# Two transformer layers on one core: GLA's backward pass handed out over attention heads

## The chip, the cores and the metric

One Trainium2 chip, one of its cores. The metric is device time of one execution in microseconds, as a median over runs. The engines are TensorE (PE, with its weight load as PEld), VectorE (DVE), ScalarE (ACT), GpSimd (POOL) and SyncE (SP), which issues most of the transfers.

## The reference

Two layers over 2048 latent tokens and 256 context tokens of width 1024. Each layer normalizes, projects to 3104 columns, lets four head groups work side by side, gates each, and projects back:

```
pl = split_proj(h_l @ w_in);  pc = split_proj(h_c @ w_in)
a = gla_mixer(...)      # gated linear attention, both directions
b = fourier_mix(...)    # 2-D Fourier transform, then w_f
c = swa_mixer(...)      # banded attention: 128-token blocks, neighbours, context, a sink logit
d = na_mixer(...)       # neighbourhood attention on the 32 x 64 grid, plus context
x = x + gate * (concat([a*silu(a_g), b*silu(b_g), c*silu(c_g), d*silu(d_g)]) @ w_out)
```

GLA runs a recurrence `S_t = diag(a_t) S_{t-1} + k_t^T v_t`, `o_t = q_t S_t` forward and backward over context and latent tokens, adds the two outputs, and takes an RMS norm per head of 64.

## The kernel before

All is fp32. Projections split each operand into a high and a low part and sum three matmuls (`mm3`, lines 218 to 222): their PSUM tiles are `ps` (input projections) and `pso` (output projection). The 2304 tokens are 9 pieces `s` of 256, or 18 tiles `T` of 128; the pieces go in three groups T1 = 0, 1, 2; T2 = 3, 4, 5; T3 = 6, 7, 8.

A layer (`trunk`, from line 1198) projects group by group and runs GLA's forward direction and the local part of both (`gla_fast`). For each tile it leaves in HBM a record `so[T]` of 642 columns: the output so far (0 to 256), the backward update (256 to 512), the decayed queries (512 to 640) and two decays. `gla_guard` then reads a flag and branches (line 639) past a slow path. After it:

- `gla_bwd` (line 646) walks the 18 tiles from the last to the first, context ahead. A tile's record `brec` is loaded; the state `sbk` of the tiles gone by is scaled (`sbe`, DVE), multiplied by the queries (`pob`, PE, in the one PSUM tile of tag `y`), added to the output (DVE). Then come a square (`bsq`, ACT), a sum (`gss`) and a scale (`ms`, both DVE), a power (`rs`, POOL, line 191), the norm's weight (`won`, POOL), a product (`bsq`, DVE), two transposes (`pyt`, PE, a tile of the two-buffered PSUM pool of tag `m`), a copy (`by`, ACT) and a store. One more DVE operation carries the state on. In layer 1 the two context tiles only carry the state on.
- `fnet` (line 689) transforms the Fourier group: 16-point transforms on DVE (`fft16`, lines 765 to 806, tiles `v`, `sd`, `fo`), then matmuls `px` into `XT`, then `pab` into `yT`.
- the last two projections of T3, `cq` and `dq` (`pst` are their transposes).
- `attention` (line 1181) takes a list of phases, makes one item of each head, and hands the items to `pipeline` (line 876), which places an item's parts a fixed number of items apart: `load`, scores `pse` (PE) in a single PSUM tile of tag `s`, bias and minimum (`S`, `am`, DVE), exponential (`S`, ACT), transposes `ppt` (PE, tag `m`), their copies `pt`, and for two heads together `py` (PE, tag `y`), which DVE scales into `yt`. Between heads stand items that project gates (`chunks`), reload (`redo`) or project out (`out_proj`). Layer 0 has 144 heads, layer 1 has 128.

Order on an engine is set by a scheduler: it takes what the program wrote first and lets later work that is ready fill the gaps. So projections, which come later in the program, stand between the pieces of GLA, FNet and the heads. At run time each engine keeps that order. `gla_bwd` and `fnet` share one pool, opened at line 1232 and closed before attention's.

Of the kernel before, what the change touches and what calls it, by code (L numbers as in the profile page):

```python
# [8 lines left out]
F32 = mybir.dt.float32  # L9
# [28 lines left out]
class Kern:  # L38
# [605 lines left out]
                    self.gla_slow(L, s, pool, lmask)  # L644

    def gla_bwd(self, L, pool):
        nc = self.nc
        sb = None
        won = pool.tile([128, 256], F32, tag="won", name="won", bufs=1)
        nc.sync.dma_start(won, self.a["won"][L].rearrange("(o d) -> o d", o=1).to_broadcast([128, 256]))  # L650
        for T in [1, 0] + list(range(17, 1, -1)):
            full = not (T < 2 and L == 1)
            rec = pool.tile([128, 644], F32, tag="brec", name="brec", bufs=4)
            if full:
                nc.sync.dma_start(rec[:, 0:642], self.so[T][:, 0:642])
            else:
                nc.sync.dma_start(rec[:, 256:512], self.so[T][:, 256:512])
                nc.sync.dma_start(rec[:, 640:642], self.so[T][:, 640:642])
            if full:
                o = rec[:, 0:256]  # L660
                if sb is not None:
                    po = self.py.tile([128, 512], F32, tag="y", name="pob")
                    sbe = pool.tile([128, 256], F32, tag="sbe", name="sbe", bufs=2)
                    nc.vector.tensor_scalar(out=sbe, in0=sb, scalar1=rec[:, 640:641], scalar2=None, op0=ALU.mult)
                    nc.tensor.matmul(po[:, 0:256], rec[:, 512:640], sbe, start=True, stop=True)
                    nc.vector.tensor_tensor(out=o, in0=po[:, 0:256], in1=o, op=ALU.add)
                sq = pool.tile([128, 256], F32, tag="bsq", name="bsq", bufs=3)
                nc.scalar.activation(out=sq, in_=o, func=AF.Square)
                ss = self.sm.tile([128, 4], F32, tag="gss", name="gss")
                nc.vector.tensor_reduce(out=ss, in_=sq.rearrange("p (h d) -> p h d", d=64), op=ALU.add, axis=AX.X)  # L670
                rs = self.rstd(ss, 4, 1.0 / 64, "g")
                nc.gpsimd.tensor_tensor(out=o, in0=o, in1=won, op=ALU.mult)
                nc.vector.tensor_tensor(out=sq.rearrange("p (h d) -> p h d", d=64), in0=o.rearrange("p (h d) -> p h d", d=64),
                                        in1=rs.rearrange("p (h o) -> p h o", o=1).to_broadcast([128, 4, 64]), op=ALU.mult)
                pt = self.pm.tile([128, 512], F32, tag="m", name="pyt")
                for b in range(2):
                    nc.tensor.transpose(pt[:, b * 128:b * 128 + 128], sq[:, b * 128:b * 128 + 128], self.idn)
                y = pool.tile([128, 2, 128], F32, tag="by", name="by", bufs=2)
                nc.scalar.copy(y, pt[:, 0:256].rearrange("p (b c) -> p b c", b=2))
                nc.sync.dma_start(self.y[L][T // 2][:, 0:2, (T % 2) * 128:(T % 2) * 128 + 128], y)  # L680
            s2 = pool.tile([128, 256], F32, tag="sbk", name="sbk", bufs=2)
            if sb is None:
                nc.vector.tensor_copy(out=s2, in_=rec[:, 256:512])
            else:
                nc.vector.scalar_tensor_tensor(out=s2, in0=sb, scalar=rec[:, 641:642], in1=rec[:, 256:512], op0=ALU.mult, op1=ALU.add)
            sb = s2


    def fnet(self, L, pool, ctx):
# [160 lines left out]
    def transpose_p(self, pool, S, n, rc=None):  # L850

        nc = self.nc
        out, rt = [], None
        for c0 in range(0, n, 3):
            w = min(3, n - c0)
            p = self.pm.tile([128, 4, 128], F32, tag="m", name="ppt")
            pt = pool.tile([128, 3, 128], F32, tag="pt", name="pt", bufs=10)  # L860
            for i in range(w):
                nc.tensor.transpose(p[:, i], S[:, (c0 + i) * 128:(c0 + i + 1) * 128], self.idn)  # L862
            if rc is not None and c0 + w == n:
                rd = pool.tile([128, 2, 64], F32, tag="rd", name="rd", bufs=2)
                nc.gpsimd.tensor_copy(out=rd, in_=rc.rearrange("p (h o) -> p h o", o=1).to_broadcast([128, 2, 64]))
                nc.tensor.transpose(p[:, 3], rd.rearrange("p h d -> p (h d)"), self.idn)
                rt = pool.tile([128, 128], F32, tag="rt", name="rt", bufs=2)
                nc.scalar.copy(rt, p[:, 3])
            if c0:
                nc.scalar.copy(pt[:, 0:w], p[:, 0:w])  # L870
            else:
                nc.vector.tensor_copy(out=pt[:, 0:w], in_=p[:, 0:w])  # L872
            out += [pt[:, i] for i in range(w)]
        return out, rt
# [306 lines left out]
    def attention(self, L, *phases):  # L1181


        with self.tc.tile_pool(name=f"at{L}", bufs=2) as p:
            items, self.bias = [], {}
            for ph in phases:
                if ph is None:
                    items += self.na_ctx_rows(L, p)
                elif isinstance(ph, int):
                    items += self.na(L, p, ph)  # L1190
                elif isinstance(ph, tuple):
                    run, nop = lambda f=ph[1]: f(), lambda *r: None
                    items.append((None, run, nop) if ph[0] == "before" else (None, nop, lambda r, x, f=ph[1]: x == 2 and f()))
                elif ph:
                    items += self.swa(L, p, ph)
            self.pipeline(items)

    def trunk(self):
        tc = self.tc
        first, kv, gates = ["av", "lr", "aqk"], ["bv", "ckv", "dk", "dv"], ["ag", "bg", "cg", "dg"]  # L1200
        for L in range(2):
# [28 lines left out]
            self.gla_guard(L)  # L1230
            kc.close()
            with tc.tile_pool(name=f"gb{L}", bufs=2) as p:
                self.gla_bwd(L, p)
                self.fnet(L, p, False)
            self.chunks(L, T3, ["cq", "dq"], h, ws)
            hs = {}
# [6 lines left out]
            b, f = (lambda f, *a: ("before", lambda: f(*a))), (lambda f, *a: ("after", lambda: f(*a)))  # L1243
# [139 lines left out]
```

## Time and profile before

| | us |
|---|---|
| median of 3 runs | 2963.52 |
| lowest and highest | 2957.93, 2965.28 |
| profiled execution, own time | 2951.03 |
| its span, first to last instruction | 2949.1 |
| PE busy | 2718.3 |
| DVE busy | 1609.3 |
| mean granted PE clock (share of 2.4 GHz) | 0.959 |

The profile is of one execution. Busy shares are means over stages that have different limits, so it is read by stretches: in layer 0 PE stops at the guard's branch at 615 us, the first `pab` of FNet starts at 723, the first `pse` at 773, the last `pse` ends near 1434; in layer 1 the same points are near 2099, 2213, 2264 and 2834.

### The profile page before, as it was taken

The numbers are of one execution on the slowest core, as the hardware profiler recorded it, in microseconds if no ns is written. First come the engines' busy times: TensorE is split into PE (matmuls) and PEld (weight loads), VectorE is DVE, ScalarE is ACT, GpSimd is POOL, SyncE is SP. The second block draws the span as 40 slices with busy tenths as digits, with TensorE's granted clock in tenths as the row PEclk, the third lists the DMA queues.
The fourth block names the chain that finished last, engine by engine and source line by source line (L and its number), as shares of the span: only waits on it lengthen the run. The fifth ranks groups of instructions, "written<-read, shape, count | busy, mean of one in ns | idle before, by whom it ended". The sixth has DMA issues, their size and how long they took to land. (4 is left out here: it accounts for less than half of the span.)

```text
span 2949.1 us, 55777 instructions
## 1 busy us (share of the span) xinstructions
PE 2718.3 (92%) x21206; PEld 2410.2 (82%) x21206; DVE 1609.3 (55%) x3741; ACT 1070.9 (36%) x2344; POOL 837.3 (28%) x922
## 2 busy tenths in 40 slices
PE   5989988988999999999959889999879999999998
PEld 5889878976888778887859889889768888878788
DVE  7554775557355454645484553464483646455543
ACT  3333323322344343344224323334232444444432
POOL 3233222234132121312133332332351313121222
PEclk9999988999999999999979999989999999999999
DMA  8635544245565274554464664333465654456545
GB/s 273 194 108 163 169 136 126 84 145 166 162 192 167 81 215 129 158 157 124 147 193 134 196 185 144 93 111 104 119 190 162 199 164 135 146 163 190 161 149 180
DMA packets 476681, 458.00 MB, mean 155 GB/s; under 512 B 54763, under 2 KB 355565, under 8 KB 476013
## 3 DMA queue, kind: packets, MB, share of 16 engines
q1 hardware_dynamic: 472782, 440.66, 48.9%
q0 software_dynamic: 3616, 13.64, 1.9%
q8 instruction: 170, 2.79, 0.4%
q14 instruction: 113, 0.93, 0.1%
HBM read 339.56 MB, written 114.60 MB: 154 GB/s over the span
## 5 line engine op out<-in xcount | busy, mean ns | idle before, releaser
L220 PE MATMUL ps<-whi,hh 128*128 128x256 f32 x1968 | 586.4, 298 | 34.7 <-ACT hh L258 17.2
L222 PE MATMUL ps<-whi,hl 128*128 128x256 f32 x1968 | 582.0, 296 | 10.2 <-DVE hl L259 10.2
L221 PE MATMUL ps<-wlo,hh 128*128 128x256 f32 x1968 | 580.8, 295 | 6.4 <-PEq L639 6.4
L213 POOL TENSOR_TENSOR wlo<-wraw,whi 128x512 fp32r<-128x512 f32 x208 | 280.8, 1350 | 775.7 <-ACT whi L212 735.1
L220 PEld LDWEIGHTS ps<-whi,hh 128*128 128x128 f32 x1968 | 391.9, 199 | 46.4 <-ACT hh L258 19.0
L220 PE MATMUL ps<-hh,whi 128*128 128x256 f32 x1376 | 402.5, 292 | 5.3 <-ACT ev L311 2.3
L222 PEld LDWEIGHTS ps<-whi,hl 128*128 128x128 f32 x1968 | 391.3, 199 | 18.5 <-DVE hl L259 13.9
L221 PE MATMUL ps<-hl,whi 128*128 128x256 f32 x1376 | 403.3, 293 | 0.0
L222 PE MATMUL ps<-hh,wlo 128*128 128x256 f32 x1376 | 402.4, 292 | 0.0
L221 PEld LDWEIGHTS ps<-wlo,hh 128*128 128x128 f32 x1968 | 392.4, 199 | 11.0 <-issue 8.8
L212 ACT CAST whi<-wraw 128x512 fp32r<-128x512 f32 x416 | 242.3, 620 | 378.5 <-DMA wraw<-w_in 206.9
L844 ACT ACTIVATE S<-S,am 128x641 f32<-128x641 f32 (+5 forms) x272 | 226.1, 831 | 339.1 <-DVE am L836 324.5
L220 PE MATMUL pso<-mh,whi 128*128 128x256 f32 x1088 | 316.7, 291 | 5.3 <-DVE xo L1107 2.9
L222 PE MATMUL pso<-mh,wlo 128*128 128x256 f32 x1088 | 316.2, 291 | 2.3 <-POOL wlo L213 1.8
L221 PE MATMUL pso<-ml,whi 128*128 128x256 f32 x1088 | 315.1, 290 | 0.0
L213 DVE TENSOR_TENSOR wlo<-wraw,whi 128x512 fp32r<-128x512 f32 x208 | 187.9, 907 | 170.9 <-ACT whi L212 163.4
L220 PEld LDWEIGHTS ps<-hh,whi 128*128 128x128 f32 x1376 | 265.9, 193 | 15.2 <-issue 7.9
L222 PEld LDWEIGHTS ps<-hh,wlo 128*128 128x128 f32 x1376 | 265.8, 193 | 15.1 <-issue 14.8
L221 PEld LDWEIGHTS ps<-hl,whi 128*128 128x128 f32 x1376 | 266.0, 193 | 11.4 <-issue 11.0
L830 PE MATMUL pse<-kst,q 64*128 64x256 f32 (+2 forms) x1184 | 246.6, 457 | 13.6 <-DVE am L836 12.5
L191 POOL TENSOR_TENSOR rs<-ms,mhalf 128x8 f32<-128x8 f32 (+2 forms) x140 | 171.3, 1226 | 297.5 <-DVE ms L189 288.6
L862 PE MATMUL ppt<-idn,S 128*128 128x128 f32 x1360 | 243.6, 284 | 10.4 <-DVE pt L872 5.2
(203 smaller groups left out, 4866.4 us busy)
## 6 DMA issues: line engine op xcount, KB each, us to landing
wraw<-w_in SPq DMA_DIRECT2D x288, 256.0 KB
wraw<-w_out SPq DMA_DIRECT2D x128, 256.0 KB
adaw<-ada_w SPq DMA_DIRECT2D x82, 256.0 KB
scr_g<-ev SPq DMA_DIRECT2D x68, 256.0 KB
g<-scr_g SPq DMA_DIRECT2D x34, 512.0 KB
y<-scr_y SPq DMA_DIRECT2D x34, 512.0 KB
bias<-nbias SPq DMA_DIRECT2D x48, 256.0 KB
scr_h<-x SPq DMA_DIRECT2D x22, 512.0 KB
```

Of the source, the lines that this page charges most:

```text
L191: nc.gpsimd.tensor_tensor(out=rs, in0=ms, in1=self.mhalf.to_broadcast([128, n]), op=ALU.pow)
L212: nc.scalar.copy(hi[:, k], raw)
L213: (nc.gpsimd if i % 4 else nc.vector).tensor_tensor(out=lo[:, k], in0=raw, in1=hi[:, k], op=ALU.subtract)
L220: nc.tensor.matmul(out, ah(k), bh(k), start=(k == 0), stop=False)
L221: nc.tensor.matmul(out, ah(k), bl(k), start=False, stop=False)
L222: nc.tensor.matmul(out, al(k), bh(k), start=False, stop=(k == KB - 1))
L830: nc.tensor.matmul(p[:, lo:hi], q[r], k, start=True, stop=True, tile_position=(64 * o, 0))
L844: nc.scalar.activation(out=S[:, 0:w], in_=S[:, 0:w], func=AF.Exp, scale=-1.0, bias=m[:, 0:1], accum_out=m[:, 1:2])
L862: nc.tensor.transpose(p[:, i], S[:, (c0 + i) * 128:(c0 + i + 1) * 128], self.idn)
```

## The change

`gla_bwd` no longer emits its 18 tiles at once. It returns 18 steps. A step loads the record of the next tile and computes its own; step 0 loads its own record too. `attention` hangs step k behind the last part of item 4k + 4, so that a step comes after every fourth item, from item 4 to item 72, in both layers. The tiles now come from attention's pool: `brec` has 2 buffers (was 4), `bsq` 2 (was 3), and `pt` of attention 9 (was 10). FNet stands alone in its pool. What is computed, and each instruction with its shape, is the same.

```diff
--- before.py
+++ after.py
@@ -644,19 +644,30 @@
                     self.gla_slow(L, s, pool, lmask)
 
     def gla_bwd(self, L, pool):
-        nc = self.nc
-        sb = None
+
+        nc = self.nc
+        st = {"sb": None, "rec": []}
         won = pool.tile([128, 256], F32, tag="won", name="won", bufs=1)
         nc.sync.dma_start(won, self.a["won"][L].rearrange("(o d) -> o d", o=1).to_broadcast([128, 256]))
-        for T in [1, 0] + list(range(17, 1, -1)):
+        tiles = [1, 0] + list(range(17, 1, -1))
+
+        def load(T):
             full = not (T < 2 and L == 1)
-            rec = pool.tile([128, 644], F32, tag="brec", name="brec", bufs=4)
+            rec = pool.tile([128, 644], F32, tag="brec", name="brec", bufs=2)
             if full:
                 nc.sync.dma_start(rec[:, 0:642], self.so[T][:, 0:642])
             else:
                 nc.sync.dma_start(rec[:, 256:512], self.so[T][:, 256:512])
                 nc.sync.dma_start(rec[:, 640:642], self.so[T][:, 640:642])
-            if full:
+            st["rec"].append(rec)
+
+        def step(n):
+            if n == 0:
+                load(tiles[0])
+            if n + 1 < len(tiles):
+                load(tiles[n + 1])
+            T, rec, sb = tiles[n], st["rec"].pop(0), st["sb"]
+            if not (T < 2 and L == 1):
                 o = rec[:, 0:256]
                 if sb is not None:
                     po = self.py.tile([128, 512], F32, tag="y", name="pob")
@@ -664,7 +675,7 @@
                     nc.vector.tensor_scalar(out=sbe, in0=sb, scalar1=rec[:, 640:641], scalar2=None, op0=ALU.mult)
                     nc.tensor.matmul(po[:, 0:256], rec[:, 512:640], sbe, start=True, stop=True)
                     nc.vector.tensor_tensor(out=o, in0=po[:, 0:256], in1=o, op=ALU.add)
-                sq = pool.tile([128, 256], F32, tag="bsq", name="bsq", bufs=3)
+                sq = pool.tile([128, 256], F32, tag="bsq", name="bsq", bufs=2)
                 nc.scalar.activation(out=sq, in_=o, func=AF.Square)
                 ss = self.sm.tile([128, 4], F32, tag="gss", name="gss")
                 nc.vector.tensor_reduce(out=ss, in_=sq.rearrange("p (h d) -> p h d", d=64), op=ALU.add, axis=AX.X)
@@ -683,7 +694,8 @@
                 nc.vector.tensor_copy(out=s2, in_=rec[:, 256:512])
             else:
                 nc.vector.scalar_tensor_tensor(out=s2, in0=sb, scalar=rec[:, 641:642], in1=rec[:, 256:512], op0=ALU.mult, op1=ALU.add)
-            sb = s2
+            st["sb"] = s2
+        return [lambda n=n: step(n) for n in range(len(tiles))]
 
 
     def fnet(self, L, pool, ctx):
@@ -857,7 +869,7 @@
         for c0 in range(0, n, 3):
             w = min(3, n - c0)
             p = self.pm.tile([128, 4, 128], F32, tag="m", name="ppt")
-            pt = pool.tile([128, 3, 128], F32, tag="pt", name="pt", bufs=10)
+            pt = pool.tile([128, 3, 128], F32, tag="pt", name="pt", bufs=9)
             for i in range(w):
                 nc.tensor.transpose(p[:, i], S[:, (c0 + i) * 128:(c0 + i + 1) * 128], self.idn)
             if rc is not None and c0 + w == n:
@@ -1193,7 +1205,15 @@
                     items.append((None, run, nop) if ph[0] == "before" else (None, nop, lambda r, x, f=ph[1]: x == 2 and f()))
                 elif ph:
                     items += self.swa(L, p, ph)
-            self.pipeline(items)
+            steps = {4 * k + 4: f for k, f in enumerate(self.gla_bwd(L, p))}
+
+            def wrap(i, item):
+                def last(r, x):
+                    item[2](r, x)
+                    if x == 2 and i in steps:
+                        steps[i]()
+                return item[0], item[1], last
+            self.pipeline([wrap(i, it) for i, it in enumerate(items)])
 
     def trunk(self):
         tc = self.tc
@@ -1230,7 +1250,6 @@
             self.gla_guard(L)
             kc.close()
             with tc.tile_pool(name=f"gb{L}", bufs=2) as p:
-                self.gla_bwd(L, p)
                 self.fnet(L, p, False)
             self.chunks(L, T3, ["cq", "dq"], h, ws)
             hs = {}
```

Three places in the order of instructions, before and after.

DVE, layer 0, inside FNet's second 16-point transform before the change (`sd`, `v` and `fo` are its tiles; `nsq` and `wlo` belong to projections):

```order
L765 TENSOR_TENSOR v<-v 128x128 x2
L765 TENSOR_TENSOR sd<-sd 128x384 x2
L664 TENSOR_SCALAR sbe<-sbk,brec 128x256
L685 SCALAR_TENSOR_TENSOR sbk<-sbk,brec 128x256
L189 TENSOR_SCALAR ms<-ss 128x8
L376 TENSOR_TENSOR nsq<-ps,wdq_897 128x512
L189 TENSOR_SCALAR ms<-gss 128x4
L666 TENSOR_TENSOR brec<-pob,brec 128x256
L213 TENSOR_TENSOR wlo<-wraw,whi 128x512
L795 TENSOR_SCALAR v<-sd 128x128
L768 SCALAR_TENSOR_TENSOR v<-sd 128x128
```

DVE, the first 16-point transform of layer 0 after the change:

```order
L777 TENSOR_TENSOR sd<-v 128x1024 x2
L777 TENSOR_TENSOR v<-sd 128x512 x2
L777 TENSOR_TENSOR v<-v 128x256
L777 TENSOR_TENSOR fo<-v 128x128 x2
L777 TENSOR_TENSOR v<-v 128x128 x2
L777 TENSOR_TENSOR sd<-sd 128x384 x2
L777 TENSOR_TENSOR fo<-v 128x128 x2
L780 SCALAR_TENSOR_TENSOR fo<-v 128x128 x4
L374 TENSOR_REDUCE ss<-nsq 128x8
L780 SCALAR_TENSOR_TENSOR v<-sd 128x128 x2
L807 TENSOR_SCALAR v<-sd 128x128
```

Of the eleven rows before, four are a GLA tile's; after the change the transform's rows follow one another with one row of a projection among them.

PE, some heads of layer 0, before (repeated `ps` rows left out):

```order
L830 MATMUL pse<-kst,q 128x384
L830 MATMUL pse<-kst,q 128x256
L862 MATMUL ppt<-idn,S 128x128 x3
L220 MATMUL ps<-hh_12562,whi 128x256
...
L220 MATMUL ps<-hh_12562,whi 128x256
L862 MATMUL ppt<-idn,S 128x128 x2
L866 MATMUL ppt<-idn,rd 128x128
L221 MATMUL ps<-hl_12563,whi 128x256
...
L221 MATMUL ps<-hl_12563,whi 128x256
L830 MATMUL pse<-kst,q 128x384
```

PE, layer 0 after the change, at the last block of window attention (heads 52 to 55):

```order
L878 MATMUL ppt<-idn,rd 128x128
L842 MATMUL pse<-kst,q 128x384
L842 MATMUL pse<-kst,q 128x256
L934 MATMUL py<-pt,vc 64x128 x4
L934 MATMUL py<-pt,vd 64x128 x4
L842 MATMUL pse<-kst,q 128x384
L842 MATMUL pse<-kst,q 128x256
L676 MATMUL pob<-sbe,brec 128x256
L688 MATMUL pyt<-idn,bsq 128x128 x2
L874 MATMUL ppt<-idn,S 128x128 x8
```

Before, twenty-odd and then nine `ps` stand between one `pse` and the next. Here there is none, and `pob` has `pyt` as its next neighbour, ahead of eight transposes of the heads.

PE, from the last `py` of layer 0 into layer 1, before (`p` is layer 1's norm; 204 `pso` from the first to the last):

```order
L922 MATMUL py<-pt,vd 64x128 x6
L220 MATMUL pso<-mh,whi 128x256
...
L222 MATMUL pso<-mh,wlo 128x256
L236 MATMUL p_18989<-ocol,sq 128x1
L240 MATMUL p_18989<-idn,rb 128x128
L236 MATMUL p_19016<-ocol,sq 128x1
L220 MATMUL ps<-whi,hh 128x256
```

PE, the same norm after:

```order
L220 MATMUL pso<-mh,whi 128x256
L236 MATMUL p_18989<-ocol,sq 128x1
L221 MATMUL pso<-ml,whi 128x256
...
L934 MATMUL py<-pt,vc 64x128 x4
L934 MATMUL py<-pt,vd 64x128 x6
L842 MATMUL pse<-kst,q 128x384
L842 MATMUL pse<-kst,q 128x256
L874 MATMUL ppt<-idn,S 128x128 x2
...
L240 MATMUL p_18989<-idn,rb 128x128
L222 MATMUL pso<-mh,wlo 128x256
```

Layer 1's first norms now stand among the last heads of layer 0, with `pso` between the two matmuls of one norm.

## Rows read from the trace of the kernel before

**Rows 1.** The page, part 1: busy us, share of the span, instructions.

```profile
PE 2718.3 (92%) x21206; PEld 2410.2 (82%) x21206; DVE 1609.3 (55%) x3741; ACT 1070.9 (36%) x2344; POOL 837.3 (28%) x922
```

**Rows 2.** Busy us of each engine by stretch (from:to, length), granted clock, DMA share.

```profile
615.00:723.00 108.00, 82.43 (x484) 72.81 (x484) 85.39 (x231) 27.48 (x65) 56.61 (x48) 0.89 0.61 182
...
2099.00:2213.00 114.00, 85.58 (x540) 76.66 (x539) 85.41 (x227) 27.77 (x66) 54.12 (x46) 0.90 0.60 174
...
760.00:1436.00 676.00, 659.51 (x5552) 551.74 (x5551) 353.78 (x841) 276.67 (x637) 155.87 (x238) 0.99 0.52 152
...
1472.00:1548.00 76.00, 43.67 (x292) 41.50 (x292) 61.96 (x134) 20.35 (x30) 29.25 (x28) 0.75 0.63 197
```

**Rows 3.** PE in order of time, layer 0: start, us, line, operation.

```profile
656.78 0.60 PE L725 MATMUL px<-T,fo 128*128 128x256 f32 x2
657.21 0.59 PE L723 MATMUL px<-T,fo 128*128 128x256 f32 x2
...
658.90 0.29 PE L222 MATMUL ps<-whi,hl 128*128 128x256 f32 x1
659.02 0.38 PE L677 MATMUL pyt<-idn,bsq 128*128 128x128 f32 x2
659.25 0.60 PE L665 MATMUL pob<-sbe,brec 128*128 128x256 f32 x2
659.68 0.38 PE L677 MATMUL pyt<-idn,bsq 128*128 128x128 f32 x2
```

**Rows 4.** PE's waits, 615 to 760: waiter, releaser; us, times, longest.

```profile
PE pyt L677 <- DVE bsq L673: 6.0, 4, 2.5
PE ps L221 <- PEq L639: 3.7, 1, 3.7
PE px L723 <- ACT XT L727: 3.6, 2, 2.1
PE pob L665 <- DMA brec<-scr_so: 3.5, 1, 3.5
```

**Rows 5.** PE's waits, 2098 to 2255.

```profile
PE pob L665 <- DVE brec L666: 12.2, 4, 5.3
PE pob L665 <- DMA brec<-scr_so: 4.7, 1, 4.7
PE pyt L677 <- DVE bsq L673: 3.2, 3, 1.9
```

**Rows 6.** DVE by group, 628 to 726: count, busy us, mean ns, idle before.

```profile
L673 DVE TENSOR_TENSOR bsq<-brec,rs 128x256 f32<-128x256 f32 x18 | 9.2, 509 | 2.9 <-POOL rs L191 2.9
...
L666 DVE TENSOR_TENSOR brec<-pob,brec 128x256 f32<-128x256 f32 x17 | 7.0, 411 | 2.3 <-PE pob L665 2.3
...
L189 DVE TENSOR_SCALAR ms<-gss 128x4 f32<-128x4 f32 x18 | 3.9, 218 | 0.1
```

**Rows 7.** Tile brec (min/median/max ns), then the page's part 5.

```profile
L668 ACT ACTIVATE bsq<-brec x34: 416/417/456, 628.2 to 2199.1; 128x256 f32<-128x256 f32 x34
...
L191 POOL TENSOR_TENSOR rs<-ms,mhalf 128x8 f32<-128x8 f32 (+2 forms) x140 | 171.3, 1226 | 297.5 <-DVE ms L189 288.6
```

**Rows 8.** All engines in order of time, attention of layer 0.

```profile
987.05 0.91 PE L830 MATMUL pse<-kst,q 64*128 64x384 f32 x4
...
988.11 0.88 DVE L836 CUSTOM_DVE_ANT_0 S<-pse,cmask,sink 128x640 f32<-128x640 f32 x1
...
995.48 0.91 PE L830 MATMUL pse<-kst,q 64*128 64x384 f32 x4
```

**Rows 9.** PE's waits, 1430 to 1560.

```profile
PE p L240 <- DVE rb L239: 10.2, 2, 6.0
PE ps L220 <- ACT hh L258: 5.7, 1, 5.7
PE p L236 <- DVE x L241: 5.3, 2, 3.1
```

**Rows 10.** PE's waits, 760 to 1120.

```profile
PE pse L830 <- DVE am L836: 4.8, 5, 1.6
```

## The prediction

> **What bounds the kernel now.** I read the page first. PE is busy for 92% of the span, no other engine for more than 55% [rows 1], so time is PE's work plus the moments in which PE has none. Next the table of stretches [rows 2], to see where PE loses time. In attention it loses little (layer 0: 659.5 us busy of 676). It loses much in the stretch that the change empties, from the guard to the first `pab` of FNet: 82.4 of 108 us busy in layer 0, 85.6 of 114 in layer 1, at granted clocks of 0.89 and 0.90. There DVE is the full engine: 85.4 of 108 and 85.4 of 114, against 353.8 of 676 in attention.
>
> How much PE loses there is worked out from starts of neighbouring matmuls, as a matmul's own duration includes its pipeline [rows 3]: a `ps` takes 0.12 us of PE (658.90 to 659.02), one pair of `px` 0.43, one `pob` 0.43, the two `pyt` 0.23. Layer 0 has 325 `ps` in the stretch (39.0), 32 `px` pairs (13.8), 17 `pob` (7.3), 16 pairs of `pyt` (3.7) and some 4 us of `pst` and `pg`: 68 us of work in 108, so **40 us lost**. Layer 1 likewise: 380 `ps` (45.6), 13.8, 16 `pob` (6.9), 3.7 and 4 make 74 in 114, again **40 lost**. PE's waits name about 26 and 28 us of it [rows 4, 5]; the rest is mostly the lower granted clock.
>
> Last, the waits: on the stretch's longest lists stand `pyt` behind DVE's `bsq` (6.0 us), `pob` behind the load of `brec` (3.5) in layer 0, `pob` behind DVE's `brec` (12.2) and its load (4.7), `pyt` (3.2) in layer 1 [rows 4, 5]. These are the GLA chain itself, and PE's queue is in order: what stands behind a late `pob` (the projections) waits too.
>
> **What is removed there.** Each tile puts six small operations on DVE. From 628 to 726 their six groups sum to 9.2 + 8.9 + 8.5 + 7.3 + 7.0 + 3.9 = 44.8 us busy of 86.2, first and last of them in [rows 6]; DVE overlaps neighbours a little, so some 31 to 45 us of DVE time leave each FNet stage, and with them 11 us of PE, 18 `brec` loads and 18 stores. FNet's transform then runs unbroken (first order fence). What stays are waits the change doesn't touch: the guard's branch (PE's queue, 3.7) and `px` behind XT (3.6) [rows 4].
> Bounds for the gain: at least the waits that name GLA's own tiles, 9.5 + 20.1 = 30 us; at most nearly all that is lost, 80 less the branch waits and a slow stretch behind each, about 65. I take 20 in layer 0 and 25 in layer 1: **45 us**, because DVE's other work in the stretch (about 41 us of the 86.2) then fits well beside PE's 60 to 70.
>
> **What is added in attention.** PE's 11 us per layer are the same work as before and cancel. Not cancelled is what the step does to the heads. In the new order a step is `pob`, then half a dozen items, then `pyt` standing ahead of the next heads' `ppt`. From `pob` to `pyt` runs DVE add 0.41, ACT square 0.42, DVE reduce 0.41 (7.3 over 18), `ms` 0.22, POOL pow 1.23, DVE multiply 0.51, together 3.2 us without hand-overs [rows 6, 7]. Usually 27 to 40 `ps` or `pso` (3.2 to 4.8 us), two `pse` and a `py` lie between, which covers it. With it go 18 loads and 18 stores per layer on SP's queue and two POOL operations per tile; POOL is busy for 156 of 676 us [rows 2], and no PE wait in attention names a `brec`-sized load, so I cost those at nothing; if SP's in-order queue holds up a `q` load, they turn up as `pse` behind a DMA. The smaller buffers (`brec` 2, `bsq` 2, `pt` 9) I also put at nothing: the load of tile n+1 waits for tile n-1, four heads back, and `pt` serves two tiles a head for three heads.
> For the 35 steps together, waits of `pob` and `pyt` lie between nothing and what these two cost beside FNet (30 us, above); I take **8**, since DVE is half idle here and a tile waits for DVE rather than for data.
>
> **Cover that is used up.** The filler between heads is finite. By the orders, layer 0 puts 598 `ps` between guard and last `pab` where it put 528, and 1053 instead of 833 under its first 48 heads; then about ten heads have almost none (second fence). Layer 1 runs short for about twelve heads late in attention. What such a head costs: two heads from 987.05 take 8.43 us until the `pse` at 995.48 [rows 8], with some 31 `ps` (3.7 us) between, so a head's own PE work is 2.35 us. The PSUM tile of the scores is single: `pse` at 987.05, DVE's reading of it (`S`, `am`) from 988.11 to 988.99, so the next `pse` could come after about 2.1 us instead of 4.2. Per bare head PE thus idles between 0 and 2.0 us (heads at 4.2 us as with filler, less 2.35, rounded up); I take 0.7, nearer the row, for 22 heads: **16 us**. Three GLA steps have little or nothing between `pob` and `pyt` either: 0 to 3.2 each, I take 2.5, near the chain's own length, as nothing else is left to run: **8 us**.
>
> **The layers' seam.** Because the filler is spent earlier, layer 0's projection of the first tokens now ends before its heads do. Before, 204 `pso` stand behind the last `py`, then layer 1's norms come with nothing beside them (third fence): PE 43.7 busy of 76 us at clock 0.75 [rows 2], with waits for `rb` (10.2), `hh` (5.7) and `x` (5.3) [rows 9], some 32 us of waits in all. Now the first three norms stand among the last heads. Between 0 and 32; I take **20 us**, as three of the six still run alone.
>
> **Sum.** -45 - 20 + 8 + 16 + 8 = **-33 us**. The profiled execution took 2951.0 us (span 2949.1), 12.5 us under the median of 2963.5; a difference carries over, so 2963.5 - 33 = **2930**.
>
> **Rivals.**
> *The heads absorb it.* By the table PEld is 551.7 of 676 us in attention, 82%, where PE is 98% [rows 2]: a busy PE there may still have room, and neither bare heads nor steps cost anything. Then -65, 2899. Against it: `pse` already waits for `am` (4.8 us in 360) [rows 10]. The Trainium skill ("Perfetto Trace Analysis", Identifying the Most-Contended Engine) says that weight-load busy time, not matmul busy time, tells PE's headroom; by it these 18% are real room and this rival's sum holds.
> *The heads stall (slower).* The place is the two-buffered pool of `pyt` and `ppt`: a `pyt` waiting for its DVE chain keeps the next heads' transposes behind it. It decides where filler is short, since then nothing fills the wait. Price: bare heads 22 x 2.0 = 44, three bare steps 8, the steps' waits as beside FNet 30, against -45 - 20: +17, **2980**. For it: under the first 48 heads the new order sets 22 `ps` to a head (1053 over 48) where it set 17. Against it: 8.43 us with only 4.7 of own work. The Trainium skill (same page, Optimization Strategy) reads a gap that repeats as too few buffers for the next tile; the old trace shows none such in attention (the longest is 4.8 us over five waits), so by that rule too it would have to be new.
> *Nothing is won.* FNet's stage keeps its pace through `px`, XT and loads of T, with more `ps` in it; only GLA's own waits go (-30), the seam stays, and the 32 us of costs come: +2, **2965**.
>
> **Chances.** Forecast 0.50, heads absorb 0.17, heads stall 0.17, nothing won 0.16. This kernel's measurement can't tell less than about 0.3% (9 us) from no change. The forecast's own range is 2908 to 2954; faster takes nearly all of it, all of the first rival and a little of the last: 0.66; no change 0.15; slower 0.19. The range leaves out a tenth on each side: 2897 to 2975.
>
> **What would show it.** Right: DVE below two thirds busy from guard to first `pab`, that stretch under 90 us in both layers, `sd` starting by itself; `pob` and `pyt` in attention with under 10 us of PE waits; the seam's waits at half. Wrong: PE waiting on `pyt`, or on `am` and `pt`, for 30 us or more where filler is missing; FNet's stretch still over 100 us; new waits of `pse` on DMA.

## The result and the profile after

The changed kernel takes 2996.02 us (median of four runs, 2991.27 to 3002.18), the kernel before 2961.47 beside it: ratio 1.0132, 95% interval 1.0105 to 1.0159. It is slower by 35 us where 33 us less were forecast, and lies above the range. The profiled execution's span is 2998.1 us (before 2949.1), the mean granted clock 0.951 (before 0.959).

The page's first part, after [rows 1]: PE is busy for 36 us more, though the kernel has the same 21206 matmuls.

```profile
PE 2754.6 (92%) x21206; PEld 2434.6 (81%) x21206; DVE 1601.2 (53%) x3741; ACT 1072.4 (36%) x2344; POOL 832.9 (28%) x922
```

Next the table of stretches (from:to, length, then busy us of PE, PEld, DVE, ACT, POOL, granted clock, DMA), cut at the same events in both kernels. After [rows 2]: guard to first `pab`, first to last `pse`, last `pse` to layer 1, then the first two for layer 1, and the end.

```profile
618.00:709.00 91.00, 73.80 (x491) 69.46 (x490) 48.93 (x129) 17.02 (x34) 20.91 (x15) 0.91 0.45 133
...
762.00:1508.00 746.00, 702.08 (x5694) 583.03 (x5694) 403.00 (x965) 293.08 (x674) 194.31 (x279) 0.96 0.52 151
1508.00:1630.00 122.00, 108.34 (x846) 104.70 (x844) 80.39 (x189) 41.63 (x78) 33.28 (x31) 0.93 0.62 194
2119.00:2203.00 84.00, 68.40 (x426) 61.84 (x425) 46.34 (x128) 15.87 (x31) 25.92 (x14) 0.88 0.46 134
...
2256.00:2921.00 665.00, 632.20 (x5206) 525.15 (x5208) 365.68 (x859) 273.09 (x622) 183.16 (x251) 0.97 0.57 167
2921.00:2998.00 77.00, 68.23 (x559) 65.59 (x559) 25.78 (x45) 18.37 (x33) 18.49 (x14) 0.98 0.50 156
```

Before, the stretches that [rows 2] don't have: heads of layer 0, the stretch behind them, heads of layer 1, the end.

```profile
773.00:1434.00 661.00, 644.72 (x5431) 537.36 (x5430) 348.91 (x835) 273.39 (x630) 150.58 (x231) 0.99 0.51 151
1434.00:1608.00 174.00, 141.64 (x1112) 138.31 (x1111) 98.27 (x215) 48.73 (x88) 48.54 (x45) 0.88 0.54 171
2264.00:2834.00 570.00, 561.03 (x4786) 461.71 (x4786) 315.65 (x740) 251.68 (x575) 139.57 (x212) 0.99 0.57 167
2834.00:2949.00 115.00, 105.58 (x870) 103.17 (x867) 43.08 (x65) 27.87 (x47) 30.20 (x21) 0.98 0.54 169
```

FNet's stretches are shorter, the heads are 85 and 95 us longer, what follows them 52 and 38 shorter. Part of this is work that moved. To see what was **lost**, I take from each difference 0.12 us for every `ps` or `pso` that came in or went, 0.43 for a `pob` and 0.23 for a pair of `pyt` (the prices of [rows 3]), with counts from the trace:

| stage | length, us | `ps` and `pso` | GLA's steps | lost, us |
|---|---|---|---|---|
| guard to `pab`, layer 0 | -17.3 | +64 | out, -11.0 | -14 |
| the same, layer 1 | -31.4 | -57 | out, -10.6 | -14 |
| heads, layer 0 | +84.6 | +179 | in, +11.4 | +52 |
| heads, layer 1 | +95.3 | +358 | in, +10.6 | +42 |
| behind the heads, layer 0 | -51.8 | -250 | | -22 |
| behind the heads, layer 1 | -38.4 | -312 | | -1 |
| all else | +8.0 | +18 | | +6 |

That is -28 in FNet's stage, +94 in the heads, -23 at the seam, +6 elsewhere: the profile's 49 us. Heads are where the forecast failed.

**How the heads lose.** Four windows, read for tile `ps` alone (the second column is the length, then PE's busy time with the count): 24 heads beside steps after the change, 12 heads further on, 24 heads before, and the same 24 as the first in the kernel of the third run below.

```profile
840.50:978.10 137.60, 81.56 (x560) 70.33 (x560) 8.18 (x12) 7.13 (x12) 1.00 0.55 159
1002.30:1064.90 62.60, 2.89 (x21) 2.50 (x21) 0.68 (x1) 0.60 (x1) 0.84 0.45 133
```

```profile
851.70:960.70 109.00, 57.09 (x383) 48.30 (x381) 4.84 (x8) 4.80 (x8) 1.00 0.55 160
```

```profile
826.00:937.60 111.60, 57.69 (x377) 47.78 (x376) 5.44 (x8) 4.84 (x8) 1.00 0.64 177
```

Before, a head goes by in 4.5 us with 16 `ps`. Beside the steps it takes 5.7 us with 23: at full clock, and almost without idle time (24 heads lose 10 us there, 6.6 before, at 2.35 us of own work each). That looks harmless, but it spends the projections. From 1002 us they are short (21 `ps` and 65 `pso` for 12 heads), PE has little beside the heads, and the clock is at 0.84. From 1117 to 1304 the heads are fed again (PE busy for 185.6 of 187 us, clock 1.00).

PE's waits of 978 to 1117, the 24 heads around that place:

```profile
PE pse L842 <- DVE am L848: 12.1, 4, 5.3
PE pyt L688 <- DVE bsq L684: 12.0, 4, 4.0
```

And what one of them looks like, PE in order of time (in brackets the idle time before it, and what ended it):

```profile
1030.86 0.59 PE L676 MATMUL pob<-sbe,brec 128*128 128x256 f32 x2
...
1031.71 0.91 PE L842 MATMUL pse<-kst,q 64*128 64x384 f32 x4
...
1036.34 0.91 PE L842 MATMUL pse<-kst,q 64*128 64x384 f32 x4 [2.48 <-DVE am L848]
1039.78 0.66 PE L688 MATMUL pyt<-idn,bsq 128*128 128x128 f32 x2 [2.53 <-DVE bsq L684]
1040.23 2.83 PE L874 MATMUL ppt<-idn,S 128*128 128x128 f32 x10
...
1043.20 1.65 PE L842 MATMUL pse<-kst,q 64*128 64x384 f32 x4
```

`pyt` waits for its chain; ten transposes of the heads stand behind it, and behind these the next `pse`. The four `pse` take 1.65 us after the waits and 0.91 ahead of them: the clock went to its lower level (0.50 granted from 1040 to 1043).

What DVE did meanwhile shows that the step's own length is not all of it:

```profile
1034.26 1.22 DVE L1095 TENSOR_TENSOR y<-y,g 128x1024 f32<-128x1024 f32 x1 [1.93 <-DMA y<-scr_y]
1035.40 0.88 DVE L848 CUSTOM_DVE_ANT_0 S<-pse,cmask,sink 128x640 f32<-128x640 f32 x1
1036.20 0.41 DVE L681 TENSOR_REDUCE gss<-bsq 128x4 f32<-128x256 f32 x1
```

DVE stood 1.93 us for a load of `y`, the output projection's input (one buffer, line 1080 of the kernel before). Behind it stood the heads' minimum (`S`, `am`), for which `pse` then waited, and the step's sum `gss`, on which `pyt`'s input hung. In this window three of the four waits for `am` follow such a wait for `y`, and the fourth (3.2 us) one for `brec`.

**Loss without a step beside it.** From 1304 to 1406 no step runs and the 16 heads have 24 `ps` and `pso` each, more than before the change, yet 18 us are lost. PE's longest wait there, and DVE's:

```profile
PE ppt L874 <- DVE rc L859: 4.6, 1, 4.6
DVE y L1095 <- DMA y<-scr_y: 24.2, 5, 7.3
```

From 2741 to 2788, in layer 1, eight heads with 13 each lose 16 us, again without a step:

```profile
PE ppt L874 <- DVE pt L884: 5.4, 1, 5.4
DVE y L1095 <- DMA y<-scr_y: 10.4, 2, 5.8
```

DVE's waits for `y` are not new. Inside the heads of both layers they sum to some 67 us before the change and 83 after it, and in two kernels below whose heads lose little they are 80 (no steps) and 64 (`pyt` two items later). So they don't cost by themselves; why they reach PE in these places and not there isn't shown, and no run takes them away.

### The profile page after: what moved, and what is told of

Its sections match the earlier page's. It is cut to its first block, busy times and chain, and to the rows that moved or that the text cites. A ratio compares the mean times of both kernels' runs of the same rounds, so it can differ in the third digit from the quotient of the medians.

```text
span 2998.1 us, 55561 instructions
## 1 busy us (share of the span) xinstructions
PE 2754.6 (92%) x21206; PEld 2434.6 (81%) x21206; DVE 1601.2 (53%) x3741; ACT 1072.4 (36%) x2344; POOL 832.9 (28%) x922
## 5 line engine op out<-in xcount | busy, mean ns | idle before, releaser
L221 PEld LDWEIGHTS ps<-wlo,hh 128*128 128x128 f32 x1968 | 393.2, 200 | 12.4 <-issue 10.2
L842 PE MATMUL pse<-kst,q 64*128 64x256 f32 (+2 forms) x1184 | 261.0, 466 | 32.9 <-DVE am L848 28.6
```

The costliest lines, as they stand in the source:

```text
L221: nc.tensor.matmul(out, ah(k), bl(k), start=False, stop=False)
L842: nc.tensor.matmul(p[:, lo:hi], q[r], k, start=True, stop=True, tile_position=(64 * o, 0))
```

## The experiments

**Theory A**: a step's `pyt` stands ahead of the heads' transposes in the two-buffered PSUM pool and holds the heads up; projections fill that wait, are spent, and later heads run bare. Against it stood B (the steps' work on DVE, ACT and POOL slows the heads), C (the tenth `pt` buffer), D (`pob` in the single PSUM tile of `py`) and later F (DVE waiting for records). Ratios are to the kernel before on the same chip. "Heads lost" is the measure of the table, both layers, against the kernel before: 94 after the change. DVE's waits for `y` were not among the rivals.

**C: buffers of `pt`.** Kernel before, one edit:

```diff
-pt = pool.tile([128, 3, 128], F32, tag="pt", name="pt", bufs=10)
+pt = pool.tile([128, 3, 128], F32, tag="pt", name="pt", bufs=9)
```

> The kernel before with one thing of the change alone: attention's pt has 9 buffers, not 10. Theory A (a step's two pyt transposes, queued in the two-buffered PSUM pool ahead of the heads' transposes, hold the heads up while their chain runs; projections fill the wait and are used up, and later heads run without any): pt is not the place, 2961 us within 9, heads of layer 0 in 655 to 668 us. Rival B (the steps' own work on DVE, ACT and POOL slows the heads): the same. Rival C (the heads lack the tenth pt buffer): slower by 25 us or more, 2986 and up.

2951.82 us, ratio 0.9997 (0.9977 to 1.0018), heads of layer 0 in 663.7 us. C falls.

**No steps.** `steps` is replaced by 34 stores of a constant:

```diff
-steps = {4 * k + 4: f for k, f in enumerate(self.gla_bwd(L, p))}
+steps = {4 * k + 4: bare(T) for k, T in enumerate([1, 0] + list(range(17, 1, -1))) if T >= 2 * L}
```

> The changed kernel without GLA's backward pass: its loads, its arithmetic and its transposes are left out, and a constant is stored in its place at the same 34 places. It leaves out 22 us of PE work. Theories A and B: heads back to about 661 and 570 us, FNet's stage as in the changed kernel (88 to 94 and 81 to 87 us from the guard to the first pab); before 2961, less 22 of work, less 28 that FNet's stage loses less, so 2911, between 2900 and 2925. Rival C (buffers): heads still 30 us or more too long, 2945 and up.

2900.91 us, ratio 0.982 (0.9791 to 0.985), heads 658 and 567 us, 9 us lost there. FNet's stretches are 89 and 85 us: what the stage wins is some 30 us, and the heads lose little without the steps.

**`pyt` two items later, and one.** A step is cut behind the product `bsq`; the rest is a function of its own, with `delay` 2 or 1:

```diff
+                st["late"] = lambda: out(T, sq)
...
-            steps = {4 * k + 4: f for k, f in enumerate(self.gla_bwd(L, p))}
+            for k, (f, g) in enumerate(self.gla_bwd(L, p)):
+                steps[4 * k + 4], steps[4 * k + 4 + delay] = f, g
```

> Each step cut in two: pyt, its copy and its store come two items after the rest of the step, all else as in the changed kernel. Theory A: pyt finds its input ready and no longer holds the heads' transposes; no group of four heads without projections beside it, heads of layer 0 about 675 to 690 us (steps' own PE work 11 us and a little more filler), no long waits of pse and ppt; FNet's gain of 28 us stays: 2935, between 2915 and 2950, faster than both. Rival B (the steps' work on DVE, ACT and POOL slows the heads): the work is the same, so 2985 to 3000. Rival D (pob in the single PSUM tile of py holds the heads): the same as B.

> As the run before, but pyt comes one item after the rest of its step. In the order of instructions projections per four heads lie between: about 60 to 96, with three heads nearly bare. Theory A: between the two, 2940 to 2965. Rivals B and D: 2985 to 3000.

Two later: 2951.37 us, ratio 0.9994 (0.9978 to 1.001). One later: 2955.43, ratio 1.0007 (0.9989 to 1.0025). Against the changed kernel's 1.0132 both win some 40 us with the same work on every engine and `pob` in the same tile, so B and D can't carry the loss by themselves. `pyt`'s place in PE's queue and its turn in the PSUM pool moved together; which of the two counts isn't shown. The stretches of the first (heads of both layers, and behind layer 0's):

```profile
750.00:1427.00 677.00, 653.90 (x5448) 542.54 (x5450) 387.16 (x940) 283.50 (x664) 183.61 (x267) 0.99 0.55 159
1427.00:1604.00 177.00, 142.44 (x1091) 137.77 (x1092) 97.37 (x214) 48.36 (x88) 45.81 (x44) 0.87 0.52 163
...
2234.00:2833.00 599.00, 585.36 (x4897) 481.71 (x4899) 351.95 (x838) 262.13 (x607) 167.92 (x244) 0.99 0.60 173
```

Heads are back at 677 and 599 us and clock 0.99, and lose 23 us instead of 94 (36 with one item). The 24 heads of the window above pass in 111.6 us with 377 `ps`. What was forecast beyond, 2935 (2915 to 2950), didn't come: some 20 us stay lost in the heads, and the stretch behind layer 0's heads is 177 us again. The seam's gain was the other face of the spent projections. Its trace once more:

> The kernel of the run with pyt two items later, once more, for its trace on this chip beside the next: 2951 us within 9.

One run, 2943.38 us (before on that chip 2953.76), 19 us lost in the heads.

**A step after every second item** (`2 * k + 4` for `4 * k + 4`).

> The changed kernel with a step after every second item, so that all 18 stand in items 4 to 38, before layer 0's window attention runs short of projections. The steps are whole, as in the changed kernel. In the order, layer 0 has 13 bare heads from head 40 on, all behind the last step; layer 1 has none. Theory A, with the loss at heads that are bare while steps stand among them: layer 0's heads some 710 to 730 us, layer 1's 620 to 650; 2960 to 2980, slower than before by less than half of what the changed kernel is. Rival B (the steps' work on DVE, ACT and POOL slows the heads): the same work in half the heads, 2990 or more.

2975.8 us, ratio 1.0084 (1.005 to 1.0118): heads 695 and 637 us (710 to 730 had been expected in layer 0), 44 lost. In layer 0, 24 heads with 193 `ps` and `pso` among them, the last of the steps at the window's start:

```profile
987.00:1087.00 100.00, 86.13 (x655) 62.66 (x654) 56.65 (x136) 43.58 (x105) 26.12 (x43) 0.90 0.50 148
```

100 less 56.4 of own work, 23.2 of projections and 0.9 of the steps: 19.5 lost, 0.8 a head. B had said 2990 or more.

**`pob` in another PSUM tile:**

```diff
-po = self.py.tile([128, 512], F32, tag="y", name="pob")
+po = self.ph.tile([128, 512], F32, tag="h", name="pob")
```

> The changed kernel with pob in the PSUM tile of tag h, which the projections' transposes (pst) use, so that pob never holds py; pyt stays in m. In the order, projections then wait behind the steps: 31 heads of layer 0 and 27 of layer 1 are bare, most of them among steps, and 1225 pso are left for the tail of layer 1 where the changed kernel leaves 498. Theory A: it prices a bare head among steps: at 1.7 us lost each (the 41.6 us lost over 24 heads of layer 0 after the change) some 100 us lost in attention, 2990 to 3040. Rival D (pob in py's tile is what holds the heads): faster than the changed kernel by 20 us or more, 2970 or less.

2992.77 us, ratio 1.0147 (1.0108 to 1.0185). As priced in time, but not in place: heads lose 55 us, not 100. Thirty-two heads with seven `pob`, nine pairs of `pyt` and 48 `ps` among them:

```profile
830.00:938.00 108.00, 94.76 (x792) 64.09 (x786) 73.40 (x206) 52.61 (x134) 27.64 (x56) 0.98 0.56 153
```

108 less 75.2, 5.8 and 5.1 for the steps: 22 lost, 0.7 a head, at clock 0.98. No wait of PE for `pyt` is in this window, nor in that of the run before. So bare heads can pass for 0.7 to 0.8, even with steps among them; where PE also waits for `pyt`, 978 to 1117 after the change, it is 1.6 (38 us over 24 heads). The projections that `pob` displaced run at the end: 179 us behind layer 1's last `pse` for 1225 `pso`. D isn't tested cleanly by this, since tag h belongs to the projections. And since `pob`'s tile or the new order may be what took the wait for `pyt` away, D can still have a part where `pyt` stands early.

**F: DVE waiting for records.** After the change DVE waits long for `brec`, one row of its waits (before: 6.1 us in 8 places):

```profile
DVE sbe L675 <- DMA brec<-scr_so: 57.7, 27, 5.5
```

A third buffer, in the changed kernel and with `pyt` two later:

```diff
-rec = pool.tile([128, 644], F32, tag="brec", name="brec", bufs=2)
+rec = pool.tile([128, 644], F32, tag="brec", name="brec", bufs=3)
-pt = pool.tile([128, 3, 128], F32, tag="pt", name="pt", bufs=9)
+pt = pool.tile([128, 3, 128], F32, tag="pt", name="pt", bufs=7)
```

> The changed kernel with 3 buffers for brec (was 2) and 7 for pt (was 9, for the room). PE's order stays nearly as it is: the same heads bare, pyt where it was. Theory F, new: with two buffers a record is loaded only when the step two tiles back is done, DVE has the next sbe queued right behind, and waits 57.7 us in 27 places for the load with the heads' minima behind it (6.1 us before); this is a second loss beside pyt's place. If F is large: DVE's wait for brec falls below 20 us, heads shorter by 20 us or more in sum, 2965 to 2978. If theory A is all: DVE's wait falls as well but the time stays, 2985 to 3000.

> pyt two items later, and 3 buffers for brec, 7 for pt. Theory F: of the some 20 us that heads still lose over the kernel before with pyt moved, ten or more go, 2928 to 2942. If DVE's wait for the records lies beside PE's work: 2951 as with pyt moved alone.

2994.02, ratio 1.0116 (1.0095 to 1.0138), and 2953.39, ratio 0.9993 (0.9979 to 1.0007). Inconclusive, as the waits stayed and only moved to the next instruction:

```profile
DVE sbk L696 <- DMA brec<-scr_so: 51.3, 23, 6.4
```

So the state was tied to the step ahead:

```diff
-sbe = pool.tile([128, 256], F32, tag="sbe", name="sbe", bufs=2)
+sbe = pool.tile([128, 256], F32, tag="sbe", name="sbe", bufs=1)
-s2 = pool.tile([128, 256], F32, tag="sbk", name="sbk", bufs=2)
+s2 = sb if sb is not None else pool.tile([128, 256], F32, tag="sbk", name="sbk", bufs=1)
```

> The changed kernel with one buffer for sbe (was 2) and the state sbk updated in place: DVE then can't take up a step's record before the step ahead has had its pob, by when the record has long landed. PE's order keeps the bare heads and pyt's place (498 pso left for the end, as in the changed kernel). If DVE's waits for records are a second cause (theory F): they fall from 57.7 us to under 10, and the time to 2965 to 2980. If pyt's place is all (theory A): they fall and the time stays, 2985 to 3000.

> pyt two items later, with the same two edits. F: of the 19 to 23 us that the heads still lose there over the kernel before, ten or more go, ratio to before 0.990 to 0.996. A alone: the ratio stays at 0.999 (0.997 to 1.001).

2992.62, ratio 1.0141 (1.0108 to 1.0174), and 2958.04, ratio 1.0016 (1.0 to 1.0032). Now the waits are gone:

```profile
DVE sbe L675 <- DMA brec<-scr_so: 4.5, 1, 4.5
```

and the time is what it was, within the runs' noise of some 13 us. F falls as a cause of the time. Within the kernel something did move: in the first of the two the heads lose 76 us and not 94, and the seam's gain is 13 and not 23, as 141 fewer `pso` stand among layer 0's heads.

**FNet's buffers.** What of FNet's loss had stayed? The longest of PE's waits after the change, guard to first `pab`, of layer 0:

```profile
PE px L735 <- ACT XT L739: 6.7, 2, 5.2
```

and of layer 1:

```profile
PE px L735 <- DMA T<-tdft: 5.8, 4, 4.6
```

`v`, `sd`, `fo` have one buffer and `T` two, so FNet's second half can't start while the first is in work. The room that GLA's tiles left takes doubles (`sd`, `fo` and `yT`, which shares their room, go with `v`):

```diff
-v = pool.tile([128, 16, 128], F32, tag="v", name="v", bufs=1)
+v = pool.tile([128, 16, 128], F32, tag="v", name="v", bufs=2)
...
-T = pool.tile([128, 384], F32, tag="T", name="T", bufs=2)
+T = pool.tile([128, 384], F32, tag="T", name="T", bufs=4)
```

> pyt two items later, and FNet's own buffers widened with the room that GLA's tiles left: its table T 4 buffers (was 2), v, sd and fo two (was 1). Only FNet's stage should move. The waits there for T (5.8 us in layer 1 after the change) go, and some of those for XT (6.7 and 2.8): each stage shorter by 3 to 10 us, 2935 to 2948. If what is left there (26 us lost in each layer) is the branch, the serial chain of px and XT in one PSUM tile and the lower granted clock behind them: no change, 2951.

> The kernel before with FNet's table T in 4 buffers (was 2), nothing else: does the widened T alone give what the widened version gave? v, sd and fo can't be doubled there, GLA's tiles take the room. Waits for T are 5.8 us in the kernel before: 2940 to 2953. 2935 or less would say that the move is not needed for the gain.

2930.0 us, ratio 0.9926 (0.9899 to 0.9953), more than the expected 2935 to 2948, against 2951.62, ratio 0.9987 (0.9974 to 1.0) for T alone in the kernel before. The stage's stretches:

```profile
613.00:688.00 75.00, 61.42 (x400) 57.42 (x399) 47.87 (x126) 14.88 (x30) 20.13 (x13) 0.91 0.49 142
2093.00:2162.00 69.00, 58.84 (x392) 55.62 (x391) 45.10 (x123) 13.79 (x28) 18.54 (x12) 0.93 0.51 151
```

By the table's measure the stage loses 45 us less than before the change, where the move alone gave 28.

**All together:** `pyt` three items later and the wide FNet, with three `brec` buffers or with the state in place.

> A version from all of it: pyt three items later, 3 buffers for brec and 7 for pt, and FNet's buffers widened as two runs before. FNet's stages as there (74 and 69 us from the guard to the first pab). If F holds 2910 to 2926, if not 2930 as there.

> pyt three items later, FNet's buffers widened, the state in place, brec with 2 and pt with 9 buffers. As the version of three items later with 3 brec buffers (2923, ratio 0.990) within 9 us if the waits lie beside PE's work; 2905 to 2914 if F holds.

2922.68 us, ratio 0.9903 (0.988 to 0.9925), and 2922.75, ratio 0.9904 (0.9879 to 0.9929). Both beat the kernel before by 1%, and, by the ratios, the changed kernel by more than 2%.

## Why the prediction was wrong, point by point

- **FNet's stage, -45 taken: mis-sized, -28.** DVE did fall to 54% busy in the stretch (48.9 of 91), the 11 us of PE work left with the steps, and both stretches are near or under the 90 us named. But the sum took 45 of the 80 us that PE lost in both layers for GLA's fault. 26 stay lost in each layer: the branch, `px` behind XT and T, and a clock of 0.91 and 0.88. The bound's own lower end, the waits that name GLA's tiles (30), was near the number. "DVE's other work then fits well beside PE's" left out that it is a serial chain through single-buffered tiles; doubling them, with four buffers for `T`, gave the 45.
- **The seam, -20: right in size (-23), wrong as a separate gain.** Its waits [rows 9] fell from 5.7, 10.2 and 5.3 us to these (PE's waits, 1410 to 1630):

```profile
PE ps L220 <- ACT hh L258: 3.0, 1, 3.0
...
PE p L240 <- DVE rb L239: 1.1, 2, 0.8
PE p L236 <- DVE x L241: 0.8, 1, 0.8
```

  It comes with the spent projections: where the heads keep them (`pyt` two later), the seam is 177 us as before. A term can't be booked without the loss that pays for it.
- **Steps' waits where there is filler, +8; bare heads, +16; bare steps, +8: here the prediction failed**, 32 against 94. Taking 2.35 us a head, 0.12 a `ps` or `pso`, and 0.66 a step: layer 0's heads from 978 to 1117 lose 38, those from 1304 to 1406 lose 18, layer 1's from 2741 to 2788 lose 16 and from 2862 to 2921 lose 12, 84 in all, where such heads lost some 17 before (6.6 over 24 heads, for the 63 here). That is 67 for these places, against 24 forecast, and some 27 for all other heads, against 8. Two steps of the sum failed. It added bare heads and bare steps as two small terms: from 978 to 1117 the wait for `bsq`, ten transposes and a `pse` behind it, and the clock's fall come together, and a head loses 1.6 us and not 0.7. And it let heads lose only where filler is missing, with DVE free to read the scores at once ("the next `pse` could come after about 2.1 us"): the other three windows, 46 of the 84 us, have no step in them, and heads lose 1.1, 2.0 and 0.8 us there, in the first two while DVE stands for `y`. The price of a bare head, 0.7, was met in three places (0.7 and 0.8 in two runs; 0.8 in the last window here).
- **The rival "the heads stall" is what happened** in the main: moving `pyt` out of its early place takes 58 to 75 of the 94 us away. Its 82 us of costs, with FNet's true -28 and the seam's -20, make +34, or 2997; measured are 2996. That this agrees so well is partly luck: its 38 us for waits of the steps stand against 12.0 us in which `pyt` waits for `bsq` in the heads (four times, all in layer 0), and part of the loss lies where filler was not short. I gave it 0.17, and put against it that a head takes 8.43 us for two with only 4.7 of own work. That room is real at full clock with nothing waiting ahead; it wasn't there behind a queue that stood (1.6 us lost a head). The evidence for it, 22 `ps` to a head where 17 stood before, was in the order and should have been followed to its end: heads that pass with more filler each were here heads that were being held (5.7 us a head for 4.5).
- **Costed at nothing, rightly in time:** the buffers of `pt` (ratio 0.9997) and of `brec`. Yet `brec` with 2 buffers did make DVE wait 57.7 us; little of it showed in PE, and taking it away didn't change the time. SP's loads and stores and POOL's work were not tested by themselves.
- **The rival "the heads absorb it"** fell: the heads lost 94 us more, and with `pyt` later still 19 to 36.
- Of the signs named as "wrong", the first came (PE behind `pyt` and `am` where filler is missing); new waits of `pse` on DMA did not (2.8 us in one place).

The Trainium skill ("Perfetto Trace Analysis", Optimization Strategy) says that interleaving stages whose fullest engines differ may help, which describes this move: DVE-bound GLA into PE-bound attention. The runs agree as far as FNet goes, and show a condition: with `pyt` in the heads' queue the move cost 35 us, with it three items later and FNet widened it won some 30.

Still open: the 10 us and more by which heads lose more with `pyt` two or three items later (19 and 23, and 25 to 32 in the kernels that change buffers too) than without steps (9). DVE's waits for records are excluded; a PSUM tile of `pyt`'s own wasn't tried, and neither was a second buffer for `y`, whose loads held DVE where heads lost most.

## What to carry to other kernels

A chain laid into a pipeline should not hold a rotating buffer and a place in an in-order queue while it is still computing (the runs moved both together): emit its last piece, on the shared engine and in the shared pool, a few items later, when its input is ready. Filler that stands between the pieces hides such a hold and pays for it later: count filler per item along the whole order, and where the count rises in one place, look for where it runs out. Then see what else stands in the helper engine's queue: a load that it waits for holds chain and heads alike. A stage that a move empties gives back what its own serial chain allows, not all that was lost in it; look at its buffers once there is room.

## What was unexpected of the hardware

The granted clock fell in the middle of attention, behind two waits of 2.5 us: the same four `pse` went from 0.91 to 1.65 us, and over 1002 to 1065 us the mean was 0.84, where it had been 1.00 beside the fed heads. It made the holds dearer than their waits. The 32 bare heads of the run with `pob` in tag h kept 0.98. And the waits of one in-order engine can weigh very differently: DVE's 57.7 us for `brec` could be taken away without a change of the time that the runs can tell, while single waits of 2 to 7 us for `y` stood ahead of PE's longest stops. In layer 0's heads DVE was busy for only 54% of the time (403 of 746 us).
